# A decoder step on one core: the copy of the first expert matrix is paced by stage

## The chip, the cores and the metric

The program runs on one core of a Trainium2 chip. The core has a matrix engine (PE, with its weight loads PEld), a vector engine (DVE), a scalar engine (ACT), a general engine (POOL), an engine that mostly issues transfers (SP), and 16 DMA engines that all of their transfers share. Each engine works through its own instructions in order; semaphores tie them together. The metric is the device time of one execution in microseconds, lower is better; a kernel's time is the median of several executions. One execution is also taken by the hardware profiler.

## The reference

One layer of a hybrid decoder for 256 prompt tokens and 64 sample tokens (320 columns in all), model width 2048, everything in fp32.

```python
def layer(x, mem_k, mem_v, ...):
    m, ... = mixer(rmsnorm(x, norm_mix), ...)     # h = xn @ w_in (2048 x 11296), SSD scan and short conv,
    x = x + m                                      # then [y_ssd ; y_sc] @ w_out (4096 x 2048)
    x = x + mem_attend(rmsnorm(x, norm_mem_q), mem_k, mem_v, w_mem_q, w_mem_o)
    x = x + peer(rmsnorm(x, norm_ffn), w_peer_q, sub_keys, peer_u, peer_v)

def peer(xn, wq, sub_keys, u, v):                  # 16384 experts of one neuron each
    ...                                            # the 16 best experts of each of 8 heads: ids eid, gates g
    act = gelu(einsum('td,tkd->tk', xi, u[ei]))
    out = einsum('tk,tkd->td', gi * act, v[ei])
```

The keys and values of 256 memory tokens are computed for the prompt (`w_mem_k`, `w_mem_v`) and read from a cache for the eight sample sequences. `u` (peer_u) and `v` (peer_v) are matrices of 16384 x 2048 numbers, 134 MB each.

## The kernel before

**Units.** Every weight matrix is streamed from memory through one machinery (`Stream`, L58). A unit is a piece of weights of 128 x 512 numbers. A transfer of 512 KB on SP's queue brings two units into a room of the tile W (L362 for 256-column panels; there are four rooms). ACT copies a unit to a rounded high part H, DVE subtracts to make the low part L (`split`, L261; seven buffers each), and PE multiplies with high and low parts of the activations: twelve matmuls of 128 x 320 a unit in the panels (L386 to L388, or L1261 to L1263 in `panel`). The loads are written three units ahead of the splitting (`WA`), and the splitting up to six units ahead of the matmuls (`GD`). `pop` (L105) writes the matmuls of the oldest unit; after each of them it lets side jobs advance by a step. The order of PE, ACT and DVE is the order in which the program writes; POOL's is chosen by a scheduler until the expert stage, written out behind it.

**Stages.** Keys and values of the prompt (128 units, to about 200 us), input projection `w_in` (352 units), the two halves of the output projection `w_out` (128 units, to about 1128 us on ACT), query panels `w_mem_q` and attention (to about 1350 us), the output panels of the attention `w_mem_o` (from the last quarter of panel `o0` on, L1595, to about 1440 us), expert queries `w_peer_q`, and from about 1570 us the two products with all experts of u and then v.

**The copy.** The prompt's product with u needs u turned. The kernel reads u in an order that DVE can turn cheaply. To have it so in memory, it copies peer_u into the buffers `u_d` (32 buffers, 128 pieces of 1 MB) by transfers from memory to memory on ACT's DMA queue (L583). They are issued by the generator `ordered_rows` (L573), which hangs on the stream as `steady`: `pop` asks it for one step after each unit (L117). The first 36 steps do nothing. From then on each step adds a share to a counter, and when the counter has reached 1, a piece is issued. The share is 0.12 for 100 steps and 0.272 after. In the expert stage SP reads `u_d` back into W (L2007). Before it, `open_p` (L1603) runs the generator to its end, should pieces be left.

**What stands around it.** `open_kv` (L1186) and `next_load` ask for blocks of the cache in the second half of `w_out`, and `kv_free` asks for further ones whenever a room is free; these transfers go through POOL. `residual_in` (L1546) loads the residual into XN at the start of the output panels; `evac_next` (L1126) adds a finished panel to it.

Of the kernel before, what the change touches and what calls it, by code (L numbers as in the profile page):

```python
# [164 lines left out]
def wait(n):  # L165
    for _ in range(n):
        yield 1
# [11 lines left out]
def step(ctx, tc, ins, outs, dbg=None, stop=None):  # L179
# [79 lines left out]
    strm = Stream(WA, g=GD, a=2)  # L259
# [245 lines left out]
    def x_norm():  # L505
        yield from wait(2)
        gb = gain_rows(norm_mix[0])
        yield from wait(2)
        for b in range(2):
            yield from norm_T(x_prompt[0, b * P:(b + 1) * P], P, gb, AH, AL, slice(b * P, b * P + P))  # L510
        yield from norm_T(x_sample.rearrange("b l d -> (b l) d"), TS, gb, AH, AL, slice(TP, T))
# [22 lines left out]
    def vectors():  # L534
        nc.sync.dma_start(WDT.rearrange("p (k h) -> p k h", h=NH),
                          w_in[0][:, C_DT:C_DT + NH].rearrange("(k p) h -> p k h", p=P))
        nc.sync.dma_start(DTB, ssd_dt_bias[0].rearrange("(o h) -> o h", o=1).broadcast_to([P, NH]))
        nc.sync.dma_start(ALOG, ssd_a_log[0].rearrange("(o h) -> o h", o=1).broadcast_to([P, NH]))
        G.memset(D4[:, T:], 0.0)
        V.tensor_reduce(FOLD, ident.rearrange("p (j h) -> p h j", h=NH), AX.X, ALU.add)  # L540
        vecs = pM.tile([P, 512], F32, name="vecs")
        for j, g in enumerate((norm_mix[0], ssd_norm[0], norm_mem_q[0], norm_mem_kv[0], norm_ffn[0], norm_final)):
            nc.sync.dma_start(vecs[16 * j:16 * j + 16, 0:P], g.rearrange("(k p) -> k p", p=P))
        nc.sync.dma_start(vecs[0:96, P:2 * P], ssd_conv_w[0].rearrange("j (k p) -> (j k) p", p=P))
        nc.sync.dma_start(vecs[0:24, 2 * P:3 * P], ssd_conv_b[0].rearrange("(k p) -> k p", p=P))
        nc.sync.dma_start(vecs[0:48, 3 * P:4 * P], sc_conv_w[0].rearrange("j (k p) -> (j k) p", p=P))
        yield from wait(2)
        pv = ps("pv")
        transpose(pv[:, 0:96], vecs[0:96, 0:P])
        transpose(pv[:, 96:192], vecs[0:96, P:2 * P])  # L550
        transpose(pv[:, 192:216], vecs[0:24, 2 * P:3 * P])
        transpose(pv[:, 216:264], vecs[0:48, 3 * P:4 * P])
        V.tensor_copy(GAIN[:, 0:48], pv[:, 0:48])
        V.tensor_copy(GAIN[:, 64:96], pv[:, 64:96])
        V.tensor_copy(CW, pv[:, 96:192].rearrange("p (j k) -> p j k", j=4))
        V.tensor_copy(CB, pv[:, 192:216])
        V.tensor_copy(SW, pv[:, 216:264].rearrange("p (j k) -> p j k", j=3))
        yield 1

    def histories():  # L560
        heads_d = pM.tile([P, NH], F32, name="heads_d")
        nc.gpsimd.dma_start(heads_d, ssd_d[0].rearrange("(o h) -> o h", o=1).broadcast_to([P, NH]))
        G.memset(HX, 0.0)
        for c0, src, nrow, nk in ((0, state_ssd_conv, 24, 24), (768, state_short_conv, 16, 16)):
            rows = src[0].rearrange("b j (k r i) -> r (b j) k i", r=4, i=32)
            for r in range(4):
                nc.sync.dma_start(HX[32 * r:32 * r + nrow, c0:c0 + 32 * nk].rearrange("c (k i) -> c k i", i=32), rows[r])
            yield 1
        for h2 in range(2):
            rows = slice(64 * h2, 64 * h2 + 64)  # L570
            G.tensor_copy(DC[rows], heads_d[rows].rearrange("p (c h) -> p h c", h=2)[:, h2])

    def ordered_rows(share):  # L573
        pops = count()

        done_ = 0.0
        for i in range(P // 4):
            for b in range(4):
                while done_ < 1:
                    done_ += share[0] if next(pops) < 100 else share[1]  # L580
                    yield 1
                done_ -= 1
                nc.scalar.dma_start(u_d[i][32 * b:32 * b + 32].rearrange("p (a d) -> p a d", d=512),  # L583
                                    peer_u[0, 512 * i:512 * i + 512, 512 * b:512 * b + 512].rearrange("(a p) d -> p a d", p=32))

    strm.steady = chain(wait(36), ordered_rows((0.12, 0.272)))
    side = strm.side(chain(x_norm(), vectors(), histories()), 0.3)
    for w, dst in ((w_mem_k, p_mem_k), (w_mem_v, p_mem_v)):
        d2 = dst[0, 0].rearrange("m h d -> m (h d)")
# [11 lines left out]
    strm.then(lambda: drain(side))  # L601
    strm.then(strm.sides.clear)
    strm.then(pMs.close)


    pS = pSs = DN = AN = ACN = DD = ACS = EE = BC = REP = DR = MB = CX = HS = HC = NX = NU = None
# [956 lines left out]
    for n in range(5 * nk + LAG):  # L1563
# [15 lines left out]
        if n == nk + LAG + 3:  # L1579
            steps.append(lambda: strm.room.update(a=3))  # L1580
    strm.then(lambda: strm.room.update(g=Q_ROOM))
    strm.ahead = Q_AHEAD
    def out_units(c):
        return gemm_units(w_mem_o[0], 256 * c, 256, RH, RL, T, lambda m, pt, c=c: evac_o(2 * c + m, pt))
# [6 lines left out]
            strm.add(*u)  # L1591
    strm.ahead = WA
    strm.then(lambda: strm.room.update(g=GD))
    strm.then(residual_in)
    for u in o0[12:] + o1[6:] + [u for c in range(3, 8) for u in out_units(c)]:  # L1595
        strm.add(*u)
# [763 lines left out]
```

## Time and profile before

| | us |
|---|---|
| time, median of 3 runs (3081.41, 3093.15, 3099.3) | 3093.15 |
| time of the profiled execution | 3081.4 |
| its span, first to last instruction | 3079.7 |
| first and last issue of a copy | 78.7, 1054.2 |
| first and last read of the copied matrix | 1552.7, 2341.2 |

The profile has a page with the busy time of each engine and 40 slices of the span, and views that answer questions on the trace: the waits (which engine waited at which line for what, in us, how often, and the longest), windows (busy time and number of instructions of each engine in a stretch of time, with the granted clock, the busy share of the DMA engines and what they moved), the DMA queues (q1 is SP's, q10 ACT's, q0 POOL's), and the instructions of a line or tile, with the time from a transfer's issue to its landing.

### The profile page before, as it was taken

The page shows a single profiled execution, that of the slowest core. Times are in us where ns is not written, and L with a number is a line of the kernel's source. Part 1 is how long each engine was busy: PE and PEld are TensorE (multiplying, and loading weights), DVE is VectorE, ACT ScalarE, POOL GpSimd, SP SyncE. Part 2 cuts the span into 40 slices and gives each one's busy share as a digit, 9 for nine tenths or more (in the row PEclk, how much of TensorE's full clock was granted, in tenths as well). Part 3 has the DMA queues.
Part 4 walks back from the last instruction along what each step waited for, and adds up shares of the span by engine and source line. Part 5 has one row for each costly group of instructions (what it writes and reads, how often), then busy time and mean ns, then how long its engine had stood idle before and what let it go on. Part 6 is the DMA issues. An engine that isn't in the chain of part 4 may idle for free.

```text
span 3079.7 us, 55322 instructions
## 1 busy us (share of the span) xinstructions
PE 3048.5 (99%) x19709; PEld 2792.0 (91%) x19709; DVE 2273.4 (74%) x4478; ACT 1587.6 (52%) x3200; POOL 1365.6 (44%) x1500
## 2 busy tenths in 40 slices
PE   9999999999999999999999999999999999999998
PEld 7889999999999999889999999888888888887886
DVE  5556866666566556656878899989885888887986
ACT  6545643434454444444554544776665555555555
POOL 0011221111110012310358999989886656555653
PEclk9999999999999999999999999999999999999999
DMA  8888899999999868965966888879998999998996
GB/s 277 288 271 307 301 333 322 314 331 306 356 323 350 294 191 259 255 229 158 242 212 208 299 310 319 307 286 322 334 335 270 340 349 353 326 340 314 344 314 220
DMA packets 445321, 909.19 MB, mean 295 GB/s; under 512 B 43336, under 2 KB 252400, under 8 KB 419572
## 3 DMA queue, kind: packets, MB, share of 16 engines
q1 hardware_dynamic: 316372, 543.31, 51.6%
q0 software_dynamic: 60656, 227.34, 22.1%
q10 hardware_dynamic: 68016, 135.01, 12.8%
q8 instruction: 154, 2.52, 0.3%
q14 instruction: 123, 1.01, 0.1%
HBM read 849.44 MB, written 190.05 MB: 338 GB/s over the span
## 4 chain that ended last, share of the span: by engine, by line
PE 85%; DVE 4%; issue 3%; DMA 3%; POOL 3%; ACT 1%; SPq 0%; DVEq 0%; ACTq 0%; POOLq 0%
PE pg L386 11%; PE pg L388 11%; PE pg L387 11%; PE pu L2056 8%; PE acc L2227 6%; PE acc L2228 6%; PE acc L2226 6%; PE pu L2057 4%; PE pu L2063 2%; PE pu L2062 2%; PE pu L2061 2%; POOL L L2037 2%; PE pgate L1959 2%; PE pg L333 2%; PE pg L335 1%
## 5 line engine op out<-in xcount | busy, mean ns | idle before, releaser
L263 ACT ACTIVATE H<-W 128x512 fp32r<-128x512 f32 x1312 | 795.7, 628 | 686.7 <-PE acc L2228 253.6
L264 DVE TENSOR_TENSOR L<-W,H 128x512 fp32r<-128x512 f32 x1312 | 900.6, 715 | 334.9 <-ACT H L263 328.7
L2037 POOL TENSOR_TENSOR L<-tt,H 128x512 fp32r<-128x512 f32 x511 | 646.9, 1298 | 60.2 <-ACT H L2034 54.5
L386 PE MATMUL pg<-AH,H 128*128 128x320 f32 x1664 | 522.3, 314 | 0.0
L388 PE MATMUL pg<-AH,L 128*128 128x320 f32 x1664 | 514.3, 309 | 0.0
L387 PE MATMUL pg<-AL,H 128*128 128x320 f32 x1664 | 514.1, 309 | 0.0
L2227 PE MATMUL acc<-L,wt 128*128 128x512 f32 x1024 | 398.6, 389 | 3.0 <-DVE L L264 3.0
L2226 PE MATMUL acc<-H,wt 128*128 128x512 f32 x1024 | 398.5, 389 | 0.4 <-DVE at L2070 0.4
L2228 PE MATMUL acc<-H,wt 128*128 128x512 f32 x1024 | 398.4, 389 | 0.0
L2034 ACT ACTIVATE H<-tt 128x512 fp32r<-128x512 f32 x512 | 308.9, 626 | 143.6 <-DVE tt L2025 123.4
L2025 DVE STREAM_TRANSPOSE tt<-W 128x512 f32<-128x512 f32 x512 | 338.3, 691 | 59.3 <-POOL L L2037 56.4
L2056 PE MATMUL pu<-XP,H 128*128 128x512 f32 x1035 | 371.3, 399 | 0.0
L386 PEld LDWEIGHTS pg<-AH,H 128*128 128x128 f32 x1664 | 313.0, 188 | 2.0 <-issue 0.5
L387 PEld LDWEIGHTS pg<-AL,H 128*128 128x128 f32 x1664 | 312.6, 188 | 1.8
L388 PEld LDWEIGHTS pg<-AH,L 128*128 128x128 f32 x1664 | 312.3, 188 | 0.0
L2057 PE MATMUL pu<-XP,L 128*128 128x256 f32 x1104 | 297.1, 279 | 0.2 <-POOL L L2037 0.2
L2179 POOL TENSOR_TENSOR at<-at,G 128x108 f32<-128x108 f32 x192 | 171.9, 908 | 241.0 <-DMA at<-act_d 211.9
L2063 PE MATMUL pu<-XP,L 128*128 128x256 f32 x944 | 269.4, 285 | 3.1 <-POOL L L2037 2.7
L2061 PE MATMUL pu<-XP,H 128*128 128x256 f32 x944 | 267.8, 284 | 0.2 <-ACT H L2034 0.2
L2062 PE MATMUL pu<-XP,H 128*128 128x256 f32 x944 | 267.0, 283 | 0.0
L2227 PEld LDWEIGHTS acc<-L,wt 128*128 128x128 f32 x1024 | 192.2, 188 | 43.7 <-DVE L L264 4.1
L2056 PEld LDWEIGHTS pu<-XP,H 128*128 128x128 f32 x1035 | 194.3, 188 | 40.0
(523 smaller groups left out, 6101.9 us busy)
## 6 DMA issues: line engine op xcount, KB each, us to landing
u_d<-in_peer_u_dram ACTq DMA_DIRECT2D x128, 1024.0 KB, 8.6
W<-u_d SPq DMA_DIRECT2D x128, 1024.0 KB, 6.8
W<-in_peer_v_dram SPq DMA_DIRECT2D x256, 512.0 KB, 6.5
W<-in_w_in_dram SPq DMA_DIRECT2D x176, 512.0 KB, 7.4
W<-in_w_out_dram SPq DMA_DIRECT2D x64, 512.0 KB, 6.7
W<-in_w_mem_k_dram SPq DMA_DIRECT2D x32, 512.0 KB, 5.7
W<-in_w_mem_v_dram SPq DMA_DIRECT2D x32, 512.0 KB, 6.0
W<-in_w_mem_q_dram SPq DMA_DIRECT2D x32, 512.0 KB, 6.2
```

Source lines behind the costliest of these rows:

```text
L263: S.activation(h, src, AF.Copy)
L264: V.tensor_tensor(l, src, h.bitcast(F32), ALU.subtract)
L386: PE.matmul(out, hv[:, j, c0:c1], ah[:, k, 0:n], start=st, stop=False)
L387: PE.matmul(out, hv[:, j, c0:c1], al[:, k, 0:n], start=False, stop=False)
L388: PE.matmul(out, lv[:, j, c0:c1], ah[:, k, 0:n], start=False, stop=sp)
L2025: V.transpose(tt.rearrange("p (k a i) -> p k a i", a=4, i=32), box["x", i].rearrange("p (a k j) -> p k a j", a=4, k=16)[:, 4 * q:4 * q + 4])
L2037: G.tensor_tensor(l, src, h.bitcast(F32), ALU.subtract)
L2056: PE.matmul(*wide, start=k == 0, stop=False)
L2057: PE.matmul(pu[:, 0:TP], lv[:, j], PP["xp"][:, 0, k], start=False, stop=False)
L2226: PE.matmul(out, th, h, start=j == 0, stop=False)
L2227: PE.matmul(out, th, l, start=False, stop=False)
L2228: PE.matmul(out, tl, h, start=False, stop=j == P - 1)
```

## The change

The two shares of the generator are taken out of its argument; it now reads `pace["copies"]`, which the stream sets at places in the program: 0.12 at the start as before, 0.21 behind the last unit of keys and values, 0 at the start of the attention stage, 0.36 just before `residual_in`.

```diff
+    pace = dict(copies=0.12)
+
-    def ordered_rows(share):
-        pops = count()
+    def ordered_rows():
...
                 while done_ < 1:
-                    done_ += share[0] if next(pops) < 100 else share[1]
+                    done_ += pace["copies"]
                     yield 1
...
-    strm.steady = chain(wait(36), ordered_rows((0.12, 0.272)))
+    strm.steady = chain(wait(36), ordered_rows())
...
     strm.then(pMs.close)
+    strm.then(lambda: pace.update(copies=0.21))
...
     strm.then(lambda: strm.room.update(g=Q_ROOM))
+    strm.then(lambda: pace.update(copies=0.0))
...
     strm.then(lambda: strm.room.update(g=GD))
+    strm.then(lambda: pace.update(copies=0.36))
     strm.then(residual_in)
```

Counted in weight units that ACT has split, the pieces stand as follows: before, piece 11 at unit 133, piece 102 at 472, piece 128 at 568. With the change, piece 11 at 133, piece 102 at 566, piece 111 at 609; then none until piece 112 at 696, and piece 128 at 740. `w_out` ends at unit 608.

ACT's order near the end of `w_out`, before the change (H is a split of weights, BH and sq prepare the next activations, `u_d` is a piece of the copy):

```order
L263 ACTIVATE H<-W 128x512 x3
L583 DMA u_d_119<-in_peer_u_dram 512x1x512
L263 ACTIVATE H<-W 128x512
L296 ACTIVATE BH<-XF,GAIN 128x320
L291 ACTIVATE sq<-XF 128x320
L296 ACTIVATE BH<-XF,GAIN 128x320
L291 ACTIVATE sq<-XF 128x320
L263 ACTIVATE H<-W 128x512 x3
L583 DMA u_d_119<-in_peer_u_dram 512x1x512
L263 ACTIVATE H<-W 128x512 x5
```

Here the copy ends, 40 units before the stage does. With the change the last rows of the stage, up to the first tiles of the attention, are these:

```order
L263 ACTIVATE H<-W 128x512 x3
L584 DMA u_d_115<-in_peer_u_dram 512x1x512
L263 ACTIVATE H<-W 128x512 x4
L584 DMA u_d_115<-in_peer_u_dram 512x1x512
L263 ACTIVATE H<-W 128x512
L296 ACTIVATE BH<-XF,GAIN 128x320
L291 ACTIVATE sq<-XF 128x320
L296 ACTIVATE BH<-XF,GAIN 128x320
L291 ACTIVATE sq<-XF 128x320
L263 ACTIVATE H<-W 128x512 x3
L263 ACTIVATE H<-W 128x4x4x32
L584 DMA u_d_115<-in_peer_u_dram 512x1x512
```

The copy now goes on until the first unit of the query panels, four to five units from piece to piece where it was three to four.

At the output panels ACT's order before the change was this (XN is the residual, `pso` the last result of the attention):

```order
L263 ACTIVATE Rh_15018<-pso 128x4x64
L263 ACTIVATE H<-W 128x512 x11
L296 ACTIVATE BH<-XN,GAIN 128x320
L288 ACTIVATE acc<-XN 128x320
L296 ACTIVATE BH<-XN,GAIN 128x320
```

With the change it is this:

```order
L263 ACTIVATE Rh_15001<-pso 128x4x64
L263 ACTIVATE H<-W 128x512 x8
L584 DMA u_d_115<-in_peer_u_dram 512x1x512
L263 ACTIVATE H<-W 128x512 x2
L584 DMA u_d_116<-in_peer_u_dram 512x1x512
L263 ACTIVATE H<-W 128x512
L296 ACTIVATE BH<-XN,GAIN 128x320
L288 ACTIVATE acc<-XN 128x320
L296 ACTIVATE BH<-XN,GAIN 128x320
```

A piece now stands behind every two or three units, seventeen in all, the first one eight units behind the attention's last result.

POOL's scheduler places a few of its instructions otherwise. At the start of the attention its order was, before the change (`x_d` is the write of the residual, krh and krl are rooms for the cache):

```order
L1149 DMA krh_12634<-in_cache_mem_k_dram 64x4x256 x2
L1196 DMA x_d<-XF 128x640
L1149 DMA krl_12635<-out_dram 32x8x128 x4
L1149 DMA krh_12636<-in_cache_mem_k_dram 64x4x256 x2
L1149 DMA krl_12637<-in_cache_mem_k_dram 64x4x256 x2
```

and with the change:

```order
L1151 DMA krh_12617<-in_cache_mem_k_dram 64x4x256 x2
L1151 DMA krl_12618<-out_dram 32x8x128 x4
L1151 DMA krh_12619<-in_cache_mem_k_dram 64x4x256 x2
L1151 DMA krl_12620<-in_cache_mem_k_dram 64x4x256
L1198 DMA x_d<-XF 128x640
L1151 DMA krl_12620<-in_cache_mem_k_dram 64x4x256
```

The last write of the residual stands behind seven more loads than before.

## The prediction

> **What bounds the kernel now.** I read the page first: how full the engines are, and how full the DMA engines are over the span.
>
> ```profile
> span 3079.7 us, 55322 instructions
> PE 3048.5 (99%) x19709; PEld 2792.0 (91%) x19709; DVE 2273.4 (74%) x4478; ACT 1587.6 (52%) x3200; POOL 1365.6 (44%) x1500
> DMA  8888899999999868965966888879998999998996
> GB/s 277 288 271 307 301 333 322 314 331 306 356 323 350 294 191 259 255 229 158 242 212 208 299 310 319 307 286 322 334 335 270 340 349 353 326 340 314 344 314 220
> ```
>
> PE is busy for 99% of the span. The DMA rows show what the change is about: from the sixth to the thirteenth slice (one slice is 77 us) the engines are nearly full at 306 to 356 GB/s, then there is a dip, which holds the attention and the output panels. The copies of the first expert matrix make up much of the full part:
>
> ```profile
> u_d<-in_peer_u_dram ACTq DMA_DIRECT2D x128, 1024.0 KB, 8.6
> L583 ACTq DMA_DIRECT2D u_d<-in_peer_u_dram x128: 548/549/678, 78.7 to 1054.2; - x128
> L2007 SPq DMA_DIRECT2D W<-u_d x128: 319/320/1117, 1552.7 to 2341.2; - x128
> ```
>
> All 128 pieces are issued between 78.7 and 1054.2 us; the first is read back at 1552.7 us. So there is room of 498 us behind the last piece, and a later copy delays no reader as long as it lands before its own.
>
> A full DMA system alone costs nothing; the question is whether PE waits for it. I therefore asked what PE waited for, first from 200 to 1140 us (the rest of the input projection and both halves of the output projection, where the pace drops), then from 1140 to 1560 us (query panels, attention, output panels, expert queries).
>
> ```profile
> PE pta L685 <- DVE AN L678: 0.6, 1, 0.6
> PE ptq L256 <- POOL rep L775: 0.2, 1, 0.2
> ...
> PE pg L1262 <- DVE Rl L264: 0.8, 1, 0.8
> PE pss L1461 <- DVE qm L1333: 0.8, 2, 0.6
> PE ppp L256 <- DVE Rl L264: 0.7, 1, 0.7
> PE ppp L256 <- DVE SP L1348: 0.6, 1, 0.6
> PE pso L1386 <- DVE Rl L264: 0.3, 1, 0.3
> ```
>
> These are all the waits of PE there: 0.8 us in 940 us, and 3.2 us in the next 420 us, none for a weight or a DMA. Waits are not the only way to lose time: "busy" overlaps from one pipelined matmul to the next, so I also compared how many matmuls start in a stretch, with the copies and without them.
>
> ```profile
> core 0: us, PE busy (x) PEld busy (x) DVE busy (x) ACT busy (x) POOL busy (x), PEclk, DMA share, GB/s
> 800.00:900.00 100.00, 100.00 (x686) 98.43 (x685) 64.19 (x112) 59.67 (x114) 11.12 (x20) 1.00 0.99 336
> 930.00:970.00 40.00, 40.00 (x275) 40.00 (x274) 28.64 (x54) 22.30 (x44) 0.00 (x0) 1.00 1.05 385
> 1056.00:1140.00 84.00, 84.00 (x575) 84.00 (x574) 47.46 (x85) 38.29 (x73) 5.18 (x10) 1.00 0.57 194
> 1150.00:1350.00 200.00, 196.82 (x1777) 168.75 (x1776) 123.96 (x204) 81.13 (x187) 57.74 (x89) 1.00 0.88 261
> 1357.00:1435.00 78.00, 78.00 (x534) 78.00 (x533) 47.29 (x86) 37.97 (x72) 0.00 (x0) 1.00 0.47 149
> ```
>
> The second row is the fullest stretch with copies: 275 matmuls in 40 us, one per 145.5 ns at 385 GB/s. The third follows the last copy: 575 in 84 us, one per 146.1 ns at 194 GB/s. The last row holds the output panels: 534 in 78 us, again 146.1 ns, at 149 GB/s. The granted clock is 1.00 in all of them. PE runs at the same speed whether the DMA engines are full or half empty: **its own rate bounds these stages, not the copies**. The fourth row is the attention; it has PE's 3.2 us of waiting, but no copy falls into it before or after. One unit is twelve matmuls, so 1.75 us.
>
> **The change part by part.** No instruction is added or taken away; the 128 copies are issued at other places of ACT's order. The order of PE, DVE and SP stays the same apart from names, so only three things can cost or gain.
>
> *Less copying from 200 to 1055 us.* The pace falls from 0.272 to 0.21 pieces a unit. What it can give back on PE is its waits there, 0.8 us, and the two that it has are for small operands. The weights' lateness that does exist ends a stage earlier:
>
> ```profile
> ACT H L263 <- PE pg L387: 50.2, 47, 1.1
> ACT H L263 <- DMA W<-in_w_out_dram: 27.2, 14, 6.4
> ```
>
> From 900 to 1056 us ACT waits 27.2 us for weights, in 14 waits of at most 6.4 us, and 50.2 us in 47 waits because the seven buffers H are all full. Seven units are 12.3 us of PE's work, and a wait of 6.4 us is covered by it. The gain is between 0 and 0.8 us; I take 0.
>
> *More copying from 1055 to 1128 us.* Copies 103 to 111 now fall there: nine pieces of 1.049 MB in 73 us are 129 GB/s, beside the 194 GB/s of the row above, so 323 GB/s. The row 800 to 900 us moves 336 GB/s with no wait on PE. Cost 0. The last of them lands about 9 us after its issue at the end of the output projection; these cache loads begin just there:
>
> ```profile
> 1137.44 1.26 POOL L1149 DMA_DIRECT2D krh<-in_cache_mem_k_dram  x2 [12.20 <-ACT BH L296]
> 1138.78 0.56 POOL L1196 DMA_DIRECT2D x_d<-XF  x1
> ```
>
> On POOL the last write of XF, 0.56 us to issue, moves behind seven of these loads and ahead of the rest: seven loads issue 0.56 us earlier, the others when they did. Its data is read back at 1345 us. I take 0 for it, between a gain of 0.6 us and nothing.
>
> *The last 17 pieces beside the output panels.* ACT issues them between the 696th and the 740th weight unit, which ACT handles from 1359 to 1437 us in this run. First the issuing: 17 times 0.549 us are 9.3 us of ACT, which is busy for 37.97 of 78 us there; cover is there twice over. Then the bytes: 17 times 1.049 MB are 17.8 MB, over 78 us 229 GB/s, beside the 149 GB/s of weights: 378 GB/s. Nearest rows: 385 GB/s for 40 us with PE at full rate, and by queue in that stretch (packets, MB, share; q10 is ACT's, q1 is SP's):
>
> ```profile
> q10 hardware_dynamic: 4048, 8.03, 53.2%
> q1 hardware_dynamic: 7369, 7.32, 51.9%
> ```
>
> The weights got 183 GB/s and the copies 201 GB/s at once, so the weights had more than the 149 they need while the copies were at 88% of the new demand. At 201 GB/s the 17.8 MB take 89 us in place of 78: the copies land up to 11 us late, and nobody waits for them until far behind 1552.7 us. The weights land later too. Time from issue to landing, minimum, median and maximum, from 900 to 950 us and then from 1357 to 1435 us:
>
> ```profile
> DMA to landing us min/median/max: 7.1/9.1/17.6
> DMA to landing us min/median/max: 3.4/5.2/6.1
> ```
>
> I expect the second to come near the first, 9 us. A weight tile is issued when its room is freed, three tiles of 3.5 us ahead, so 10.5 us, and behind it are the 12.3 us of full H buffers. The first row shows 17.6 us once, with PE at full rate. Cost 0; the bounds are 0 and what the rivals below give.
>
> The first panel's sum also waits for XN, loaded just before:
>
> ```profile
> L1552 POOL DMA_DIRECT2D XN<-x_d x4: 538/544/566, 1345.2 to 1346.8; - x4
> L1128 DVE TENSOR_TENSOR XN<-XN,pg x16: 478/481/489, 1366.9 to 1443.3; 128x320 f32<-128x320 f32 x16
> DMA to landing us min/median/max: 5.6/7.0/8.5
> ```
>
> It lands by 1355.3 us at the latest, is first read at 1366.9, and the first copy comes at 1359: no meeting. The last copies land by about 1450 us, beside the loads of the expert queries, where 115 us have 220 GB/s:
>
> ```profile
> 1435.00:1550.00 115.00, 115.00 (x810) 114.72 (x809) 86.44 (x293) 57.28 (x130) 34.03 (x68) 1.00 0.85 220
> ```
>
> PE has no wait for a DMA there now; two pieces more are 2.1 MB, some 6 us of DMA time at the rates above. Cost 0.
>
> The sum on the profiled execution is 3081.4 us (its time outside, 1.7 us around a span of 3079.7) plus 0. That execution was the fastest of three, 3081.41, 3093.15 and 3099.3; what the other two spent more is not in the profile. So I carry the zero to the median: 3093, less at most 0.8 and 0.6: **3092 us**.
>
> **The rivals.** *The relief counts in the executions that I cannot see.* The other two runs took 12 and 18 us more. If that is weights coming late where the engines are nearly full, the lower pace removes it and the median comes to 3081 or, with a quieter run than the one seen, 3075. For it: ACT's 27.2 us of waiting shows that the reserve is used. Against it: at 385 GB/s nothing reached PE.
>
> *The output panels starve, by the split between the queues.* If the DMA engines gave both queues one packet each in turn while both have work, the weights (7.32 MB in 7369 packets, 993 bytes each) would get 33% beside packets of 1984 bytes, 128 of 385 GB/s, and 78 us of panels would take 91: +13 us, 3106 on the median, with the H buffers already spent. It decides if the copies' queue never runs empty. Against it: from 930 to 970 us the two queues had 1.8 packets to 1. The Trainium skill, "DMA: Bandwidth & Descriptors", section "Queues, rings and completion order", says that each engine goes round the queue rows at packet granularity; by that rule, where a record is a packet, this rival's 13 us would be paid, and the trace's 1.8 to 1 does not agree with it.
>
> *The output panels starve, by the sum.* If 385 GB/s cannot be held for 78 us and 336, as from 800 to 900 us, is the level, 42 GB/s times 78 us are 3.3 MB short. Taken wholly from the weights at 149 GB/s that is +22 us with no cover, 10 us with the 12.3 us of H buffers: 3103 to 3115, slower than before. It decides when a weight tile takes over some 20 us to land.
>
> *The change does not shift the copies.* The orders show that it does, so no chance.
>
> **How the numbers follow.** Forecast, nothing on PE: 0.70, 3092 us. Relief in the unseen executions: 0.17, 3075 to 3081. Split: 0.06, 3106. Sum: 0.07, 3103 to 3115. Half a per cent is 15.5 us, about what a measurement of this kernel can tell from no change: faster is below 3077.7, slower above 3108.6. Of the relief something under half lies below, and I add 0.02 for the spread of three runs: 0.10. Of the sum half and of the split a third lie above, with 0.03 of spread: 0.09. That leaves 0.81. The range goes from 3074 to 3107: it holds the forecast, the relief nearly whole, the split and the lower half of the sum.
>
> **What would show it.** The profile after should have 128 issues from 78.7 to about 1437 us with none between 1128 and 1359; DMA near 0.85 from 300 to 1050 us and near 1.0 from 1360 to 1440; still about 534 matmuls in the 78 us of the output panels, and PE's waits below 1 us from 200 to 1140. ACT's waits for the weights of the output projection should shrink from 27 us to under 10, with no effect. Weights landing at over 15 us in the median in the output panels, or under 500 matmuls in 78 us there, would prove me wrong on the slow side; a span more than 5 us shorter, with a stage that I called bound by PE running faster, on the fast side.

## The result, and the profile after

The kernel became slower. Its median is 3111.61 us (six runs, 3107.3 to 3118.26) against 3086.93 us of the kernel before (six runs on the same chip, 3081.41 to 3099.3). The ratio is 1.008, with a 95% interval of 1.0065 to 1.0096, so the change costs about 25 us. The profiled execution of after took 3118.3 us. These are the lines of its page that answer to those of before:

```profile
span 3116.5 us, 55315 instructions
PE 3058.8 (98%) x19709; PEld 2796.6 (90%) x19709; DVE 2269.4 (73%) x4478; ACT 1587.4 (51%) x3200; POOL 1347.7 (43%) x1500
DMA  8888799888998898978966788879998989999996
GB/s 276 288 275 288 263 290 307 283 277 290 320 300 298 276 298 237 283 250 288 241 203 222 287 313 318 311 285 323 332 332 269 337 285 361 332 347 324 334 317 211
```

The DMA load is spread as meant: the full stretch from the sixth slice on is lower, and the dip behind it is filled up. PE has lost a per cent of its share. The windows over the output panels and the stretch just behind them show where:

```profile
core 0: us, PE busy (x) PEld busy (x) DVE busy (x) ACT busy (x) POOL busy (x), PEclk, DMA share, GB/s
1357.00:1435.00 78.00, 72.49 (x486) 70.93 (x485) 40.15 (x75) 32.30 (x63) 0.00 (x0) 1.00 0.85 285
1450.00:1460.00 10.00, 9.52 (x53) 9.25 (x54) 4.76 (x9) 3.55 (x7) 0.00 (x0) 0.83 0.96 308
```

In the 78 us where before started 534 matmuls, after starts 486, though the DMA engines move only 285 GB/s, far below the 385 that before held in another stage. What PE waited for in after, first from 1128 to 1360 us (the longest wait), then from 1370 to 1480 us:

```profile
PE pg L1263 <- ACT H L263: 3.4, 1, 3.4
...
PE pg L386 <- ACT H L263: 7.0, 4, 2.0
PE pky L256 <- DMA W<-in_peer_sub_keys_dram: 4.4, 1, 4.4
```

So PE now runs dry at three places: once at the start of the attention, four times in the output panels, and once for the sub-keys, which come right behind the panels.

Every run has 19,709 recorded matmuls in the same order. So the loss can be placed by comparing the start of the n-th matmul with that of the n-th of before. The table gives how much a run falls behind in five stages (bounds by the time of before: 200, 1040, 1200, 1370, 1440, 1480, 1560 us; nothing changes from 1200 to 1370). The first 200 us differ by up to 5.6 us between runs of the same code there and are left out. The last columns compare the sum with the difference of the medians; "before" in it is 3086.93 us for after, 3085.6 us (14 runs) for e1 to e4, and 3086.11 us (24 runs) for e5 to e8.

| run | input and output projection, 200–1040 | end of it, start of the attention, 1040–1200 | output panels, 1370–1440 | sub-keys, 1440–1480 | expert queries, 1480–1560 | sum | difference of medians |
|---|---|---|---|---|---|---|---|
| after | 0.6 | 4.0 | 11.0 | 6.2 | 1.0 | 22.8 | 24.7 |
| e1 (no copy in the panels) | 2.1 | 4.5 | 0.0 | 0.0 | 1.4 | 8.0 | 5.0 |
| e2 (copies later) | 0.6 | 4.7 | 9.1 | 8.6 | 0.6 | 23.6 | 23.5 |
| e3 (half rows) | 0.6 | 3.9 | 3.2 | 9.7 | 1.0 | 18.4 | 16.4 |
| e4 (residual's write moved) | 0.5 | 1.3 | 10.2 | 7.4 | 1.0 | 20.4 | 19.7 |
| e5 (copies ahead of the sums) | 0.5 | 4.5 | 2.8 | 4.3 | 2.7 | 14.8 | 11.1 |
| e6 (e5 and e4) | 1.0 | 1.6 | 4.6 | 4.6 | 1.6 | 13.4 | 8.0 |
| e7 (one a panel) | 0.5 | 4.0 | 0.0 | 0.0 | 0.7 | 5.2 | 4.5 |
| e8 (two a panel) | 0.5 | 4.5 | 4.2 | 6.0 | 1.6 | 16.8 | 12.1 |

For after the five stages hold 22.8 of the 24.7 us. The other sums lie up to 5.4 us above the difference of the medians; each is from one execution. In e7 and e8 the share of the first 200 us is another one, and they are left out there too (e7 is 1.0 us late by then, e8 1.3). The profiled execution of after, the slowest of six, lost some 14 us more in the last products (from 2300 us to the end), which no edit here touches; e2 lost 5 there, the others nothing. This is not counted as part of the change.

**How the output panels lose it.** ACT's instructions of after around the end of a panel, start, duration and, in brackets, the idle time before:

```profile
1399.05 0.56 ACT L296 ACTIVATE BH<-XN,GAIN 128x320 fp32r<-128x320 f32 x1 [1.06 <-DVE XN L1130]
1399.06 0.55 ACTq L584 DMA_DIRECT2D u_d<-in_peer_u_dram  x1
...
1399.76 0.55 ACTq L584 DMA_DIRECT2D u_d<-in_peer_u_dram  x1
1399.88 1.66 ACT L263 ACTIVATE H<-W 128x512 fp32r<-128x512 f32 x3
1400.95 0.62 ACTq L584 DMA_DIRECT2D u_d<-in_peer_u_dram  x1
1401.44 2.18 ACT L263 ACTIVATE H<-W 128x512 fp32r<-128x512 f32 x4
1411.90 0.63 ACT L263 ACTIVATE H<-W 128x512 fp32r<-128x512 f32 x1 [8.28 <-PE pg L388]
```

and SP's loads of weights in the same stretch (four issues, 1401.25 to 1404.9 us):

```profile
1401.25 5.53 SPq L362 DMA_DIRECT2D W<-in_w_mem_o_dram  x4
```

ACT works in order and stands at BH, which needs the finished panel. When it goes on, everything behind BH goes out at once: three copies in 2 us (3.1 MB), seven splits in 4 us, and, because the splits free all four rooms of W together, four weight loads (2.1 MB) just behind the copies. Then ACT waits 8.28 us for the next weight (the bracket names PE, whose wait had long been over; from 1405 to 1411 us SP's queue moved 0.58 MB, a little over the first of these loads with its 0.52 MB). The same place of before, with no copies:

```profile
1401.58 0.56 ACT L296 ACTIVATE BH<-XN,GAIN 128x320 fp32r<-128x320 f32 x1 [1.06 <-DVE XN L1128]
...
1402.41 2.18 ACT L263 ACTIVATE H<-W 128x512 fp32r<-128x512 f32 x4
1405.08 0.63 ACT L263 ACTIVATE H<-W 128x512 fp32r<-128x512 f32 x1 [0.50 <-PE pg L387]
1406.84 0.63 ACT L263 ACTIVATE H<-W 128x512 fp32r<-128x512 f32 x1 [1.13 <-PE pg L387]
```

Before, ACT does four splits, finds H full, and goes on at PE's pace, one split each 1.76 us: three units of reserve survive the wait at BH. In after all seven H are empty when ACT goes on, and they are empty again one panel later: a panel never gets back what it started without.

What the two queues carry while both have work, from 1422 to 1427 us in after (packets, MB, share; q10 is ACT's copies, q1 SP's weights):

```profile
q10 hardware_dynamic: 557, 1.11, 67.9%
q1 hardware_dynamic: 492, 0.50, 30.3%
```

Packets go about one to one (557 to 492), but a packet of the copy has 2 KB and one of the weights 1 KB. So the weights get 100 GB/s (0.50 MB in 5 us) and the copies 222. The Trainium skill, "DMA: Bandwidth & Descriptors", section "Queues, rings and completion order", says that an engine goes round its queue rows at packet granularity; counted in the profile's records, this trace agrees from 1422 to 1427 us.

The share is not all of it. From 1402 to 1405 us this is the only queue that moves anything:

```profile
q10 hardware_dynamic: 573, 1.14, 101.2%
```

The first load of weights had been issued at 1401.25 us, but its first packet comes at 1405.4, 4.2 us behind the issue. In before, with no copy ahead, the load issued at 1403.77 us has its first packet 1.0 us behind. The other three bursts of after show 4.2 to 4.3 us, e7 below, with one copy ahead, 2.2 us. So the loads lose twice: they start late, and then they get the smaller share. Why a load waits while only copies move is not shown.

### The profile page after: what moved, and what is told of

Its sections match the earlier page's. It is cut to its first block, busy times and chain, and to the rows that moved or that the text cites. A ratio compares the mean times of both kernels' runs of the same rounds, so it can differ in the third digit from the quotient of the medians.

```text
span 3116.5 us, 55315 instructions
## 1 busy us (share of the span) xinstructions
PE 3058.8 (98%) x19709; PEld 2796.6 (90%) x19709; DVE 2269.4 (73%) x4478; ACT 1587.4 (51%) x3200; POOL 1347.7 (43%) x1500
## 3 DMA queue, kind: packets, MB, share of 16 engines
q10 hardware_dynamic: 68016, 135.01, 12.9%
## 4 chain that ended last, share of the span: by engine, by line
PE 80%; DMA 5%; issue 5%; DVE 5%; POOL 4%; ACT 1%; SPq 0%; DVEq 0%; POOLq 0%; ACTq 0%
PE pg L386 10%; PE pg L388 10%; PE pg L387 10%; PE pu L2060 7%; PE acc L2231 6%; PE acc L2230 6%; PE acc L2232 6%; PE pu L2061 4%; POOL L L2041 3%; PE pgate L1963 2%; PE pu L2067 2%; PE pu L2066 2%; PE pu L2065 2%; PE pg L1263 2%; PE pg L334 1%
## 5 line engine op out<-in xcount | busy, mean ns | idle before, releaser
L2183 POOL TENSOR_TENSOR at<-at,G 128x108 f32<-128x108 f32 x192 | 158.2, 838 | 264.8 <-DMA at<-act_d 231.1
L2230 PEld LDWEIGHTS acc<-H,wt 128*128 128x128 f32 x1024 | 192.9, 188 | 46.0 <-issue 4.6
```

Source lines behind the costliest of these rows:

```text
L2230: PE.matmul(out, th, h, start=j == 0, stop=False)
```

## The experiments

All start from after. Where an expectation speaks of the cost of the output panels, the table's columns for the panels and the sub-keys together answer it (17.2 us in after).

**e1, no copy in the panels.** The pace is raised so that all 128 pieces are out before the attention.

```diff
-    strm.then(lambda: pace.update(copies=0.21))
+    strm.then(lambda: pace.update(copies=0.25))
```

> Pace 0.25 instead of 0.21 behind the keys and values, so that all 128 pieces are issued by weight unit 601 and none is left for the output panels; POOL's scheduler then puts the last write of the residual where it stood before the change. Theory (the loss lies at two places: about 19 us in the output panels and at the loads of the keys beside them, about 4 us where ACT waits for the last write of the residual): both go, time 3087 within 6, ratio to before 0.998 to 1.002, DVE's and ACT's weight unit 760 within 2 us of before's 1483 us. Rival (the loss comes from more copying in the second half of the output projection, up to its end): the 4 us at its end stay or grow, since the copies are denser there than with 0.21, ratio 1.002 to 1.004. Rival of the relief (a lower pace gains in executions not profiled): below 3081.

Measured: 3090.57 us (ten runs), ratio 1.0015 (1.0004 to 1.0026). The output panels and the sub-keys cost nothing, so the 17 copies there cause those 17.2 us. The other half of the expectation failed: the write stands at its old place on POOL and ACT waits 2.01 us ahead of pm in place of 7.14, but 4.5 us are lost from 1040 to 1200 us all the same. The 0.25 has a small price of its own, as the rival had it, in the second half of the output projection: two copies now fall into each panel there, and ACT waits from 1060 to 1145 us

```profile
ACT H L263 <- DMA W<-in_w_out_dram: 24.8, 4, 7.4
```

in four waits of up to 7.4 us, the same picture as in after's output panels; PE is 1.9 us late by 1140 us, and behind it PE waits twice for H, 1.3 us each; what makes H late there was not followed further.

**e2, the copies later in the burst.** Three copies per panel, some units behind BH rather than right behind it.

```diff
-    strm.then(lambda: pace.update(copies=0.36))
...
+    late = {1: 0.9, 3: 0.0, 9: 1.5, 11: 0.0, 17: 1.5, 19: 0.0, 25: 1.5, 27: 0.0, 33: 1.5, 35: 0.0, 41: 1.5, 43: 0.0}
...
+        if j in late:
+            strm.then(lambda r=late[j]: pace.update(copies=r))
```

> The same 17 pieces beside the output panels, but three issued in the back part of each panel's burst of splits (behind the fifth and sixth of eight) instead of directly behind the sums of a finished panel. Theory (three copies go out 1 to 2 us before four weight loads and take the DMA engines from them; ACT then waits 8 us a panel): weight loads come first, the four panels of 16.5 us come back to 14 to 14.8 us, of the 19 us 3 to 8 are left, time 3095 to 3103. Rival (378 GB/s in all is more than the DMA engines give over the panels): the same bytes in the same time, the panels stay at 16 us or more, time 3108 to 3115.

Measured: 3109.1 us (five runs, from 3095.69 to 3115.26), ratio 1.0057 (1.0036 to 1.0079); panels and sub-keys 17.7 us, no recovery. The theory's figure failed, since the edit moved the copies by units and hardly by time:

```profile
1405.98 0.55 ACTq L584 DMA_DIRECT2D u_d<-in_peer_u_dram  x1
...
1407.33 0.55 ACTq L584 DMA_DIRECT2D u_d<-in_peer_u_dram  x1
1407.84 1.66 ACT L263 ACTIVATE H<-W 128x512 fp32r<-128x512 f32 x3
1416.92 0.63 ACT L263 ACTIVATE H<-W 128x512 fp32r<-128x512 f32 x1 [7.43 <-DMA W<-in_w_mem_o_dram]
```

All seven splits of a burst take 4 us. The three copies stand behind one, two and four of them and leave 1.05 to 2.40 us behind the start of BH (1404.93 us), where those of after left 0.01 to 1.90 behind it, so about 1 us later at most. They still meet the weight loads (1407.12 to 1410.73 us here). The run does not tell the theories apart; it says that an order within a burst is not a spacing in time.

**e3, half rows.** The pieces from the 112th on are copied in rows of 1 KB rather than 2 KB, in two issues each.

```diff
+                n = 512 if 4 * i + b < 111 else 256
+                for e in range(0, 512, n):
+                    nc.scalar.dma_start(u_d[i][...][:, :, e:e + n], peer_u[0, ..., 512 * b + e:512 * b + e + n]...)
```

> The last 17 pieces as 34 transfers with rows of 1 KB in place of 2 KB, same bytes, same places. Theory with an even split by packets between the two queues: the weights, whose rows are 1 KB, get half of the bytes and not a third while both queues have work, about 180 GB/s in place of 108; the panels fall from 16.5 us to 14.5 to 15.5 us, time 3098 to 3106. Rival (sum of bytes): no gain, rather a loss from smaller packets, 3111 to 3118. Rival (split by bytes): no change, 3112.

Measured: 3102.04 us (four runs), ratio 1.0048 (1.0029 to 1.0067). The panels fall from 11.0 to 3.2 us; the sub-keys rise from 6.2 to 9.7. With both queues at work, from 1413 to 1418 us:

```profile
q1 hardware_dynamic: 967, 0.96, 54.4%
q10 hardware_dynamic: 968, 0.96, 54.4%
```

The same bytes, at one packet each and equal rows, give the weights 192 GB/s in place of 100. So the size of a row sets the share that the weights get, and with a larger share most of the panels' loss goes. Panels and sub-keys together still cost 12.9 us in place of 17.2, and why the sub-keys lose more is not shown. The pieces are also split into twice as many issues, so the spacing changed too: the load issued at 1406.57 us has its first packet 3.0 us behind, in place of 4.2.

**e4, the residual's last write on ACT's queue.** The write of XF that POOL's scheduler had put behind seven loads no longer goes through POOL.

```diff
-        strm.then(lambda c=c: nc.gpsimd.dma_start(x1_d[:, 2 * c:2 * c + 2], XF[:, 2 * c:2 * c + 2]))
+        strm.then(lambda c=c: (nc.scalar if c == 7 else nc.gpsimd).dma_start(x1_d[:, 2 * c:2 * c + 2], XF[:, 2 * c:2 * c + 2]))
```

> As the change, but the last write of the residual goes out on ACT's queue in place of POOL's, so that no cache load stands ahead of it. Theory (ACT clears pm in memory that this write reads; behind seven cache loads it lands 6 us later, ACT stands, PE runs dry for 3.7 us): ACT's wait ahead of pm falls from 7.1 us to 1 to 3 us, weight unit 620 comes within 2 us of before's 1153.6, in place of 7 us behind it; time 3106 to 3109; the output panels stay at 16.5 us. Rival (ACT stands there because of the copies that run until the end of the output projection): wait and loss stay, 3112.

Measured: 3105.29 us (four runs), ratio 1.0068 (1.005 to 1.0087); the start of the attention costs 1.3 us rather than 4.0, the rest is unchanged. POOL's order in after, ACT's instruction that waits on it, then the same instruction in e4:

```profile
1142.70 0.63 POOL L1151 DMA_DIRECT2D krl<-in_cache_mem_k_dram  x1
1143.31 0.56 POOL L1198 DMA_DIRECT2D x_d<-XF  x1
...
1149.05 0.63 ACT L1282 ACTIVATE pm<-ident 128x512 f32<-128x512 f32 x1 [7.14 <-issue]
```

```profile
1146.88 0.63 ACT L1282 ACTIVATE pm<-ident 128x512 f32<-128x512 f32 x1 [1.82 <-DMA x_d<-XF]
```

ACT clears pm, which lies in the memory that XF leaves, so the clearing waits until the write has read XF out. In after the write is issued at 1143.31 us, 4.5 us later than in before (1138.78), ACT stands 7.14 us, and PE runs dry for the 3.4 us shown above. With the write on another queue ACT stands 1.82 us, and the bracket names the write.

**e5, the copies ahead of the sums.** Three copies per panel, issued just before ACT comes to BH, behind all splits of the burst.

```diff
+        if k >= 4 and k % 2 == 0:
+            pace.update(copies=3.0)
+            next(strm.steady, None)
+            pace.update(copies=0.0)
+            next(strm.steady, None)
...
-    strm.then(lambda: pace.update(copies=0.36))
```

> The same 17 pieces beside the output panels, three for each finished panel, now placed in ACT's order directly ahead of the sums of that panel, behind all eight splits, where the weight loads of the burst have landed and the next ones are some 6 us off. Theory (a panel's copies and its four weight loads go out together, 5.2 MB, and the weights come late because the copies share the engines just then): the panels come back to 14.1 to 14.8 us, weight units 704 to 744 cost 0 to 5 us against before in place of 17; time 3094 to 3102, with the 4 us at the start of the query panels and the key loads still there. Rival (378 GB/s in all is too much however it is laid out): panels 15.5 us or more, units 704 to 744 cost 10 us or more, 3105 to 3112.

Measured: 3097.16 us (seven runs), ratio 1.0039 (1.0021 to 1.0056). Panels and sub-keys together cost 7.1 us in place of 17.2: more than half comes back, though less than the theory had, which left 0 to 5 us. ACT's instructions show a reason:

```profile
1410.66 0.63 ACT L263 ACTIVATE H<-W 128x512 fp32r<-128x512 f32 x1 [6.82 <-DMA W<-in_w_mem_o_dram]
1410.67 1.91 ACTq L584 DMA_DIRECT2D u_d<-in_peer_u_dram  x3
...
1415.50 3.74 ACT L263 ACTIVATE H<-W 128x512 fp32r<-128x512 f32 x7
```

The copies leave at 1410.67 us, the next seven splits, and with them the next weight loads, begin 4.8 us later. Three copies are 3.1 MB, some 8 us at 385 GB/s, so they are still under way. The burst remains; it meets fewer of the copies' bytes.

**e6, e5 and e4 together.**

> The edit of the run before this one together with the last write of the residual on ACT's queue. Theory: both gains add up, units 600 to 640 cost 0 to 1.5 us and units 704 to 744 0 to 5 us against before; time 3088 to 3097. Rival (378 GB/s is too much): 3101 to 3108. A version that beats before is not expected by either: PE waited for nothing there that these copies could take away.

Measured: 3094.15 us (ten runs), ratio 1.0024 (1.0013 to 1.0036). The start of the attention costs 1.6 us in place of 4.5 in e5: the write's term comes off as in e4, and does not depend on the copies in the panels. The time is as expected, but the panels and the sub-keys cost 9.2 us, over the 0 to 5 of the expectation and over the 7.1 of e5.

**e7, one copy a panel, and e8, two.** The share at the start and that in the panels are set so that five and eleven pieces are left for the panels.

```diff
-    pace = dict(copies=0.12)
+    pace = dict(copies=0.242)
...
-    strm.then(lambda: pace.update(copies=0.36))
+    strm.then(lambda: pace.update(copies=0.13))
```

> Five to six pieces beside the output panels, about one a panel, in place of seventeen; the eleven others are moved into the keys and values (pace 0.242 there, whose own cost is read apart, from weight unit 133). Theory (what counts is the bytes that go out together at a panel's end: 1.05 MB of copies and 2.1 MB of weights): weight units 704 to 744 cost 0 to 2 us against before. Rival (any copy at that place costs in proportion): 5 to 6 us, a third of 17.

In e8 the two shares are 0.176 and 0.25.

> Eleven pieces beside the output panels, two a panel (pace 0.176 in the keys and values, 0.25 in the output panels). In all 149 and 149 GB/s, far under the 336 to 385 that the engines moved elsewhere. Theory (burst of 2.1 MB of copies with 2.1 MB of weights, split by packets; in the run with pace 0.25 in the output projection such panels took 15 to 15.5 us): weight units 704 to 744 cost 3 to 8 us against before. Rival (sum of bytes): 0 to 1 us. Rival (in proportion to the copies): 11 us.

Measured: e7 3090.6 us (ten runs), ratio 1.0022 (1.001 to 1.0033); e8 3098.16 us (six runs), 1.0034 (1.0021 to 1.0046). One copy a panel costs the panels and the sub-keys nothing, two cost 10.2 us, three 17.2. For e7 that is the theory's forecast; for e8 its 3 to 8 us were too low, and the rival in proportion to the copies, with 11, was nearer. But that rival gave e7 5 to 6 us, so it does not hold for both. Most of what is left of e7's loss is the 4.0 us of the write, whose place on POOL it shares with after. ACT's waits for weights from 1380 to 1456 us, of e7 first:

```profile
ACT H L263 <- PE pg L387: 12.8, 13, 1.1
...
ACT H L263 <- DMA W<-in_w_mem_o_dram: 4.1, 2, 2.7
```

and of e8:

```profile
ACT H L263 <- DMA W<-in_w_mem_o_dram: 27.3, 4, 7.3
```

In e7 ACT waits mostly for PE (13 waits: H is full, the reserve is back in each panel); in e8 it waits for weights as in after. So there is a point between one and two copies a panel at which the reserve no longer recovers, and a loss in each panel follows. A sum of bytes has no such point at these loads. The window of e8 over the output panels, and one of after at the end of the output projection:

```profile
1360.00:1440.00 80.00, 78.74 (x529) 77.42 (x529) 41.91 (x77) 33.05 (x64) 0.00 (x0) 1.00 0.77 254
...
1100.00:1140.00 40.00, 40.00 (x275) 40.00 (x274) 22.61 (x40) 18.01 (x35) 3.18 (x6) 1.00 0.89 316
```

e8 loses matmuls at 254 GB/s (529, where before has 548), and after loses none at 316.

No version beats the kernel before; PE sets its time at each of these places, so there was nothing for the copies to give back.

## Why the prediction was wrong

Forecast was no effect, 3092 us, range 3074 to 3107. Part of that figure was its base: the three runs' median of 3093 was 6 us above the 3086.93 of six. On the difference, which counts, it was off by 25 us. Three of its zeros failed: the moved write cost 4.0 us, the 17 copies 11.0 us in the output panels, and their last ones 6.2 us at the sub-keys.

- **PE's own rate bounds the stages before: right.** It is also why the relief could not pay.
- **Relief, 0: right.** After is 0.6 us late from 200 to 1040 us, not early. ACT's waits for weights from 900 to 1056 us fell from 27.2 to 15.1 us, with no effect on PE. The rival of a relief in unseen executions falls.
- **Copies 103 to 111 beside the end of `w_out`, 0: right.** PE loses nothing from 1040 to 1140 us.
- **"I take 0" for the moved write: wrong, 4.0 us.** The step asked when the written data is read back (1345 us) and not who waits to use XF's memory again. Seven loads on POOL ahead of it were counted as issue time only.
- **Issue time of the 17 copies hidden, and the rival by the sum of bytes dismissed: right.** ACT is at 32.30 of 78 us, and the DMA engines moved less than they had shown. The measured 3111.6 us lies within that rival's 3103 to 3115, but by coincidence: e8 loses 10.2 us at 254 GB/s.
- **"Cost 0" for the output panels, by a cover of 10.5 us and 12.3 us: wrong, 11.0 us.** This step fails in two ways. It spread copies and weights evenly over 78 us, while ACT's wait at BH bunches both into the same 6 us of each panel (1399 to 1405 us above). And it counted the H buffers as full at a moment when they are empty: the rooms of W come free only because H was empty, so the two covers are not there at once.
- **The "1.8 packets to 1", by which the packet split was put aside: misread.** That was a mean over 40 us in which now the one and now the other queue had the engines nearly to itself. In before the weights moved nearly alone from 948 to 951 us; from 928 to 932 us, around the start of the 40, both moved at once:

```profile
q1 hardware_dynamic: 988, 0.98, 92.3%
q10 hardware_dynamic: 92, 0.18, 16.0%
...
q10 hardware_dynamic: 458, 0.91, 60.4%
q1 hardware_dynamic: 462, 0.46, 33.4%
```

  Where both move at once, packets go one to one in before too (458 to 462). The rival of the split named a large part of the mechanism, at a chance of 0.06; that its 13 us lie near the measured 11.0 of the panels is in part luck. It left out the late start of the loads, and its condition, that the copies' queue never runs empty, was too strong: in after it does run empty in each panel, and the loss is made in the part of the panel where it does not.
- **XN and the first copy, no meeting: right.** PE loses nothing there until 1398.8 us.
- **The last copies beside the expert queries, "Cost 0": wrong, 6.2 us.** The last three leave at 1449 to 1450.5 us in the last burst, and the first sub-keys are loaded in the same burst, at 1454.79 us where before loaded them at 1438.14. PE reads them straight from W, with no H in between. What PE does when they are due in after:

```profile
1467.34 0.88 PE L256 MATMUL pky<-ident,W 128*128 128x128 f32 x4 [4.37 <-DMA W<-in_peer_sub_keys_dram]
...
1468.28 0.47 PE L387 MATMUL pg<-BL,H 128*128 128x320 f32 x1
1468.55 0.47 PE L388 MATMUL pg<-BH,L 128*128 128x320 f32 x1
```

  It waits 4.37 us, and the matmuls behind it start 0.27 us apart, where 0.146 was the rate of before.
- **The signs.** "Under 500 matmuls in 78 us" came true, with 486. The DMA share from 1360 to 1440 us was 0.86 and not near 1.0, and ACT's waits for weights fell to 15.1 us and not under 10. A median landing of over 15 us was no good sign: e8 lost 10.2 us at a median landing of 9.3 us, about what had been forecast as harmless.

Open: why a load's first packet comes only 4.2 us after its issue when three copies run, what of e5's 7.1 us is the copies' tail and what a burst would cost alone, and where between one and two copies a panel the point lies. More rooms of W were not tried.

## What to carry to other kernels

A background transfer that is issued from an in-order engine's queue leaves whenever that engine leaves its wait, together with all the loads that the same engine's work sets free; count bytes and buffers at that moment, not over the stage. Between two busy queues compare rows, not bytes: here the one with rows twice as long got twice the bandwidth (222 to 100 GB/s), and a load issued behind three copies began to move only 4.2 us after its issue, where it took 1.0 us without them. When a transfer is delayed, ask who waits to reuse the memory that it reads as well as who reads what it writes.

## What the runs showed of the hardware

A short stall of PE cost more than its length here. In after the waits of PE from 1370 to 1480 us are 7.0, 0.5 (not shown above) and 4.4 us, 11.9 in all, and the loss is 17.2 us. The granted clock was 0.83 from 1450 to 1460 us (0.50 from 1450.6 to 1454.0, 1.00 after that), behind a wait of at most 2.0 us, with 53 matmuls in 10 us where full rate gives about 70. The Trainium skill, "TensorE: Matmul & The Clock Gate", section "HAM oscillation — how this bites in real kernels", sets the rule that PE's idle gaps stay under about 3.4 us; the drop behind the 4.37 us for the sub-keys (0.50 from 1467.6 to 1471.0 us) agrees with it, but the drop at 1450 us follows a shorter gap, and the measurement decides.
